# Four moves in a two-layer encoder kernel: gathers, query tables, gate weights, and a second attention unit

## The chip, the cores and the metric

The kernel runs on one core of one Trainium2 chip. A core has a matrix engine (TensorE; PE in the profile, its weight loads PEld), three engines for everything else (VectorE is DVE, ScalarE is ACT, GpSimd is POOL) and a queue for transfers on SyncE (SP). They work side by side, each through its own list of instructions in a fixed order, and wait for each other by semaphores. TensorE writes only to PSUM, eight banks; everything else lives in SBUF. The metric is the device time of one execution in microseconds, lower is better.

## The reference

The input is 1024 tokens of width 1024, with 16 learned meta tokens in front. Two layers follow: a gated linear attention (layer A), then attention over one shared, compressed key and value set (layer B).

```python
h = deltanet_layer(h, valid, ...)          # A: per 64 tokens, 8 heads of 128
#   o = rms_norm(o, o_gain) * silu(gate);  h = x + o @ w_out
c = rms_norm(h, g_norm) @ w_down           # shared latent: 256 latent + 64 rotary
k = rms_norm(concat(c_kv @ w_uk, k_pe)); k = concat(k_nope, rope(k_pe)); v = c_kv @ w_uv
# layer B
z = rms_norm(h, g_norm) @ w_in             # 384 query latent, 1024 gate
q = rms_norm(rms_norm(z[:384]) @ w_uq);    q = concat(q_nope, rope(q_rope))
o = softmax(mask(q @ k.T * scale)) @ v     # chunk-causal, 8 heads
h = h + (o * silu(z[384:])) @ w_out
```

All of it is in 32-bit floats. The kernel splits each operand of a large product into a high and a low part and makes three products of it (`mm3`, lines 92 to 95), so that lines 93, 94 and 95 are the three products wherever they stand.

## The kernel before

Activations are kept transposed, features on the partitions, tokens along the free axis, in the three token chunks of `TOKC`: 272, 384 and 384 tokens, the first with the meta tokens. Weights come in by `SY.dma_start` into a tile `raw` (or `rq`, `wdr`), and `split_w` makes the high part on GpSimd (line 100 or 106) and the low part on VectorE (101 or 107). `split_ps` does the same for a PSUM result, with ScalarE for the high part.

Layer A ends with eight gate blocks, one per head (`gate`, lines 776 to 784): three chunks of 24 products, a SiLU on ScalarE after each. The heads' outputs lie in DRAM (`o_scr`), 128 tokens to a tile, and have to be normalised, transposed, multiplied by the gates and split before the output projection can read them: `gather_rows` loads a tile's rows and gates, `out_gather` scales eight head pieces on ScalarE (line 761), transposes them on TensorE into two PSUM banks of the tag `tr` (767), multiplies by the gates (770, 772) and splits (773, 774). Tile -1 is the 16 meta tokens. The first three tiles (-1, 0, 1) make up the first token chunk `oT0`, and their gathers are handed to the last gate block as the list `between`: one after each chunk. The output projection (`out_project`) follows, chunk by chunk, with the gathers of later tiles among its blocks; these loads go to a pool that lies where `hT` was, so they wait until the last gate product has read it.

Then come the latent projections (from line 944): `latent_kv(c)` makes three blocks of products with `w_down` for chunk c, `latent_q(c)` three with the query part of `w_in`. Norms need a product with a matrix of ones (lines 1009 and 1039), whose result lies in the only bank of the tag `pt` until VectorE has read it (1011 and 1013, 1041). Work that waits for a norm is put off through the list `later` and called by `soon()` after the next block. Among it is `all_tables`: the rotary tables for queries (`qC`, `qS`, scaled) and, in place, for keys (`cosS`, `sinS`). The query weights come in eight pieces of 128 rows, fetched three ahead (`fetch_wq`) and split a pair at a time between the key blocks (`query_weights`). Behind `latent_kv(2)` the weights of the first gate block of layer B are loaded and split (`load_wg`), into space that the key weights leave.

The eight gate blocks of layer B (lines 1154 to 1170) are 48 products of 512 columns each. Blocks 1 to 7 take their weights from a pool of two buffers, which lies where the latent projections' tiles were, beside the up-projection weights of the first pair of heads (`pair_weights`).

The attention (from line 1173) is in a block opened with `tc.block(schedule_with_timeline_sim=True)`: the program's order is a priority, and a scheduler orders the instructions at compile time by estimated durations. It works by units of a pair of heads and 256 tokens, four units to a pair, 16 in all. `build` makes a unit's keys (`K`, a generator of five steps: projection and copy, squares, norm in three steps), values (`VV`), queries (`Q0`, `Q1`), their rotation on GpSimd (`R0`, `R1`) and the transposes of all of them (`TK`, `TR`, `turn_q`, `turn_qr`). All of these use three PSUM banks of the tag `bd`. `scores` makes a unit's products of queries and keys and the softmax, `weigh` the product with the values. `weave` interleaves several such generators by the estimates they yield, each between two shares of the span. Unit 0 is built by itself, then in each unit's scores the next unit is built, 0.8 of it beside the first head and the rest beside the second. The last output projection follows (`out_b`).

## Time and profile before

| what | us |
|---|---|
| median of 3 runs | 1327.56 |
| lowest and highest run | 1326.98, 1329.74 |
| profiled execution, device time | 1322.61 |
| its span, first to last instruction | 1320.9 |
| TensorE busy in it | 1281.3 |
| mean granted TensorE clock | 0.993 of full |

The profile is of one execution. The page lists busy time by engine, 40 slices of the span, the chain that ended last, and the costliest groups of instructions. Behind it stands the trace, which can be asked for waits, for the instructions of a stretch in order of time, and for the busy time of engines in a stretch. In order of time, a row is start, duration, engine, line, operation, tiles and shapes, how many, and in brackets how long the engine stood idle before and what released it. TensorE's durations overlap, since its products are pipelined; the pace is the difference of two starts. The granted clock is given as a share of 2.4 GHz.

### The profile page before, as it was taken

To read this page: it belongs to the slowest core of one execution; us is meant where nothing else is said; L and a number is where in the kernel's file an instruction comes from. 1 tells how busy PE (TensorE), PEld (TensorE's weight loads), DVE (VectorE), ACT (ScalarE), POOL (GpSimd) and SP (SyncE) were. 2 spreads that over 40 slices of the span, in tenths; PEclk is the share of its full clock that TensorE was granted. 3 is DMA by queue.
4 is the path that set the end of the run, shared out by engine and by line. 5 is a ranking of instruction groups with operands and counts; after the bars stand their busy time and mean duration, and the time that the engine had idled before them with its cause. 6 is when DMAs were issued, how large, how long until landed. Compare 5 with 4: busy or idle time off the path is not lost. (4 is left out here: it accounts for less than half of the span.)

```text
span 1320.9 us, 25401 instructions
## 1 busy us (share of the span) xinstructions
PE 1281.3 (97%) x9320; PEld 1196.2 (91%) x9320; DVE 901.6 (68%) x2534; ACT 598.3 (45%) x1764; POOL 320.0 (24%) x588
## 2 busy tenths in 40 slices
PE   6999999999999999999999999989999999998999
PEld 5889989989998999999999897878999999997888
DVE  7679789978987884653556655336878878777411
ACT  6543444344435422246522321137777777775200
POOL 3141121022111101040011013214544445447000
PEclk9999999999999999999999999999999999999999
DMA  5011111111111202174543004220101100014622
GB/s 198 33 34 46 52 29 54 41 45 40 57 49 37 64 24 91 61 241 147 178 127 104 11 18 144 81 90 15 53 25 50 43 29 26 21 40 165 203 90 79
DMA packets 95822, 96.85 MB, mean 73 GB/s; under 512 B 28526, under 2 KB 77614, under 8 KB 95698
## 3 DMA queue, kind: packets, MB, share of 16 engines
q1 hardware_dynamic: 95698, 95.23, 22.9%
q8 instruction: 73, 1.20, 0.4%
q14 instruction: 51, 0.42, 0.1%
HBM read 68.19 MB, written 27.01 MB: 72 GB/s over the span
## 5 line engine op out<-in xcount | busy, mean ns | idle before, releaser
L93 PE MATMUL mm<-hT_hi,whi 128*128 128x384 f32 (+1 forms) x768 | 255.5, 333 | 4.3 <-ACT hT_hi L293 4.3
L94 PE MATMUL mm<-hT_lo,whi 128*128 128x384 f32 (+1 forms) x768 | 254.9, 332 | 0.5 <-DVE hT_lo L294 0.5
L95 PE MATMUL mm<-hT_hi,wlo 128*128 128x384 f32 (+1 forms) x768 | 254.6, 332 | 0.0
L93 PEld LDWEIGHTS mm<-hT_hi,whi 128*128 128x128 f32 x768 | 146.2, 190 | 6.3 <-issue 5.5
L94 PEld LDWEIGHTS mm<-hT_lo,whi 128*128 128x128 f32 x768 | 146.4, 191 | 2.2 <-DVE hT_lo L294 1.0
L95 PEld LDWEIGHTS mm<-hT_hi,wlo 128*128 128x128 f32 x768 | 146.8, 191 | 1.1 <-issue 0.4
L100 POOL TENSOR_SCALAR whi<-raw 128x512 fp32r<-128x512 f32 x48 | 34.6, 736 | 165.8 <-PE mm L94 123.9
L93 PE MATMUL bd<-oTh,wf_hi 128*128 128x256 f32 (+1 forms) x192 | 61.4, 323 | 3.0 <-DVE xt L1610 3.0
L113 DVE TENSOR_TENSOR pTl<-pt,pTh 128x256 fp32r<-128x256 f32 (+2 forms) x112 | 54.7, 494 | 14.0 <-ACT pTh L112 12.8
L95 PE MATMUL bd<-oTh,wf_lo 128*128 128x256 f32 (+1 forms) x192 | 61.8, 322 | 0.0
L94 PE MATMUL bd<-oTl,wf_hi 128*128 128x256 f32 (+1 forms) x192 | 61.7, 322 | 0.0
L84 ACT ACTIVATE P<-P,mx 128x144 f32<-128x144 f32 (+3 forms) x64 | 50.6, 792 | 23.2 <-DVE mx L1448 15.0
L1610 DVE TENSOR_TENSOR xt<-bd,xt 128x256 f32<-128x256 f32 (+1 forms) x24 | 12.3, 514 | 67.9 <-PE bd L95 59.9
L396 ACT COPY z<-mm 128x384 f32<-128x384 f32 (+1 forms) x72 | 32.0, 444 | 58.3 <-PE mm L95 57.4
L1461 POOL TENSOR_SCALAR P<-P,sl 128x144 f32<-128x144 f32 (+3 forms) x64 | 52.4, 820 | 4.1
L112 ACT CAST pTh<-pt 128x256 fp32r<-128x256 f32 (+2 forms) x112 | 47.0, 427 | 12.8 <-DVE pTl L113 7.0
L101 DVE TENSOR_TENSOR wlo<-raw,whi 128x512 fp32r<-128x512 f32 x64 | 46.8, 741 | 8.4 <-POOL whi L100 8.3
L400 DVE SCALAR_TENSOR_TENSOR kn<-z,pcol,kn 128x384 f32<-128x384 f32 (+1 forms) x72 | 42.1, 585 | 15.2 <-ACT kn L398 14.3
L93 PE MATMUL sc<-h_hi,whi 128*128 128x512 f32 x128 | 50.8, 397 | 1.2 <-POOL whi L106 1.2
L95 PE MATMUL sc<-h_hi,wlo 128*128 128x512 f32 x128 | 50.6, 395 | 1.1 <-DVE wlo L107 1.1
L94 PE MATMUL sc<-h_lo,whi 128*128 128x512 f32 x128 | 50.6, 395 | 0.0
L93 PE MATMUL sc<-kn_hi,qn_hi 128*128 128x272 f32 (+3 forms) x160 | 48.0, 302 | 2.0 <-DVE mx L1448 1.5
(428 smaller groups left out, 4013.1 us busy)
## 6 DMA issues: line engine op xcount, KB each, us to landing
raw<-in_a_w_in SPq DMA_DIRECT2D x64, 256.0 KB
o_scr<-o SPq DMA_DIRECT2D x64, 64.0 KB
raw<-in_a_w_out SPq DMA_DIRECT2D x8, 512.0 KB
on<-o_scr SPq DMA_DIRECT2D x8, 512.0 KB
raw<-in_b_w_in SPq DMA_DIRECT2D x8, 512.0 KB
gb_scr<-z SPq DMA_DIRECT2D x8, 512.0 KB
gt<-gb_scr SPq DMA_DIRECT2D x32, 128.0 KB
ot_scr<-gt SPq DMA_DIRECT2D x32, 128.0 KB
```

The lines of the kernel that those rows point to most:

```text
L84: i = A.activation(out_ap, in_ap, func, **kw)
L93: TE.matmul(ps, ahi, bhi, start=first, stop=False)
L94: TE.matmul(ps, ahi, blo, start=False, stop=False)
L95: TE.matmul(ps, alo, bhi, start=False, stop=last)
L100: eng.tensor_scalar(out=hi, in0=raw, scalar1=1.0, scalar2=1.0, op0=ALU.mult, op1=ALU.mult)
L101: V.tensor_tensor(out=lo, in0=raw, in1=hi, op=ALU.subtract)
L112: A.copy(hi, ps)
L113: V.tensor_tensor(out=lo, in0=ps, in1=hi, op=ALU.subtract)
L396: A.copy(z[:, 3 + a:3 + b], gemm_T(hi, lo, c))
L400: V.scalar_tensor_tensor(out=yc, in0=z[:, a + j:b + j], scalar=col("cw", 24 * j + m), in1=yc, op0=ALU.mult, op1=ALU.add)
L1461: G.tensor_scalar(out=Pm[:, 0:n], in0=Pm[:, 0:n], scalar1=s, scalar2=1.0, op0=ALU.mult, op1=ALU.mult)
L1610: V.tensor_tensor(out=xt, in0=ps, in1=xt, op=ALU.add)
```

## The change

First, the gathers of tiles -1 and 0 both go behind the first chunk of the last gate block of layer A, that of tile 1 behind the second; behind the third there is none. Second, the tables for keys get tiles of their own (`kC`, `kS`) and stay at their place, the tables for queries are made behind `latent_q(0)`; the query weights are fetched two ahead instead of three, in two buffers, and the rotary temporaries `t1`, `t2` have one buffer instead of two. Third, the weights of the first two gate blocks of layer B are loaded and split behind `latent_kv(2)`, with one buffer for the raw weights, and blocks 2 to 7 use the other pool. Fourth, unit 0 of the attention is woven with the first part of unit 1 (`cut` at an estimate of 4100), for which `build` has an order of its own with values and queries first: by the estimates, `VV`, `Q0` and `Q1` fall into the opening, and the key steps and the rest come beside the scores of unit 0.

```diff
--- before.py
+++ after.py
@@ -821,7 +821,13 @@
 
         for t in (-1, 0, 1):
             gather_rows(t, so)
-        gate(H - 1, [first_gather(t) for t in (-1, 0, 1)])
+        gathers = [first_gather(t) for t in (-1, 0, 1)]
+
+        def first_two():
+            gathers[0]()
+            gathers[1]()
+
+        gate(H - 1, [first_two, gathers[2]])
 
 
     lps = ExitStack()
@@ -931,8 +937,8 @@
         V.memset(kpe[:, NT:NT + 1], 0.0)
         qC, qS = (cpool.tile([P, NT, ROPE], F32, name=x) for x in ("qC", "qS"))
 
-        def load_wg(pool, h):
-            raw = pool.tile([P, KT, P], F32, tag="raw", name=nm("raw"))
+        def load_wg(pool, h, raws=2):
+            raw = pool.tile([P, KT, P], F32, tag="raw", name=nm("raw"), bufs=raws)
             SY.dma_start(raw, I["b_w_in"][0].rearrange("(kt p) c -> p kt c", p=P)[:, :, QR + h * P:QR + (h + 1) * P])
             hi = pool.tile([P, KT, P], F32R, tag="whi", name=nm("whi"))
             lo = pool.tile([P, KT, P], F32R, tag="wlo", name=nm("wlo"))
@@ -965,28 +971,28 @@
                     V.tensor_tensor(out=S[:, :, x], in0=sinS[:, 0:n, x],
                                     in1=gr[:, gi:gi + 1, y].broadcast_to([P, n, hf]), op=ALU.mult)
 
-            def all_tables():
+            kC, kS = (wc.tile([P, NT + 1, ROPE], F32, name=x) for x in ("kC", "kS"))
+
+            def query_tables():
                 tables(qC, qS, 1, NT)
                 for x in (qC, qS):
                     V.tensor_scalar(out=x, in0=x, scalar1=QK ** -0.5, scalar2=None, op0=ALU.mult)
-                tables(cosS, sinS, 0, NT + 1)
-
-            kC, kS = cosS, sinS
+
             hf = ROPE // 2
             wqr = []
 
             def fetch_wq(kt):
-                wqr.append(sp.tile([P, WQ], F32, tag="rq", name=nm("rq"), bufs=3))
+                wqr.append(sp.tile([P, WQ], F32, tag="rq", name=nm("rq"), bufs=2))
                 SY.dma_start(wqr[kt], I["b_w_in"][0, kt * P:(kt + 1) * P, 0:QR])
 
             def query_weights():
                 for kt in range(KT):
                     split_w(wqr[kt], wq_hi[:, kt, :], wq_lo[:, kt, :], col("b", kt))
-                    if kt + 3 < KT:
-                        fetch_wq(kt + 3)
+                    if kt + 2 < KT:
+                        fetch_wq(kt + 2)
                     yield
 
-            for kt in range(3):
+            for kt in range(2):
                 fetch_wq(kt)
             wqs = query_weights()
 
@@ -1065,7 +1071,7 @@
                         continue
                     n, s0, i0 = len(ts), ts[0] % (NT + 1), tiles.index(ts[0])
                     s, x = slice(s0, s0 + n), pt[:k, i0:i0 + n]
-                    t1, t2 = (sp.tile([P, 3, ROPE], F32, tag=y, name=nm(y))[:k, 0:n] for y in ("t1", "t2"))
+                    t1, t2 = (sp.tile([P, 3, ROPE], F32, tag=y, name=nm(y), bufs=1)[:k, 0:n] for y in ("t1", "t2"))
                     V.tensor_tensor(out=t2, in0=x[:, :, 0:ROPE], in1=kC[:k, s, :], op=ALU.mult)
                     V.tensor_tensor(out=t1[:, :, 0:hf], in0=x[:, :, hf:ROPE], in1=kS[:k, s, 0:hf], op=ALU.mult)
                     V.tensor_tensor(out=t1[:, :, hf:ROPE], in0=x[:, :, 0:hf], in1=kS[:k, s, hf:ROPE], op=ALU.mult)
@@ -1097,7 +1103,7 @@
                 V.tensor_tensor(out=kp, in0=ps, in1=rrow[0:ROPE, a:b], op=ALU.mult)
                 soon()
                 if c == 0:
-                    later.append(all_tables)
+                    later.append(lambda: tables(kC, kS, 0, NT + 1))
                 later.append(lambda: rotary(c, kp))
 
             def latent_q(c):
@@ -1114,9 +1120,11 @@
             latent_kv(0)
             latent_kv(1)
             latent_q(0)
+            query_tables()
             latent_kv(2)
             lwd.close()
-            wg0 = load_wg(lpre.enter_context(tpool(name="wg0", bufs=1, side="right")), 0)
+            wg0 = lpre.enter_context(tpool(name="wg0", bufs=2, side="right"))
+            first_gates = [load_wg(wg0, h, 1) for h in range(2)]
             latent_q(1)
             latent_q(2)
             soon()
@@ -1154,7 +1162,7 @@
         with ExitStack() as lg:
             wg = lg.enter_context(tpool(name="wg", bufs=2))
             for h in range(H):
-                hi, lo = wg0 if h == 0 else load_wg(wg, h)
+                hi, lo = first_gates[h] if h < 2 else load_wg(wg, h)
                 z = wg.tile([P, T], F32, tag="z", name=nm("z"))
                 for half in range(2):
                     c = slice(512 * half, 512 * half + 512)
@@ -1232,7 +1240,7 @@
             return first, second, third
 
 
-        def build(u, w, r):
+        def build(u, w, r, early=False):
 
             uk_hi, uk_lo, uv_hi, uv_lo, uq_hi, uq_lo = w
             base = NM if u == 0 else 0
@@ -1245,7 +1253,7 @@
             kn_hi, kn_lo, kr = (kt_(x, [P, 2, NM + 256], KB) for x in ("kn_hi", "kn_lo", "kr"))
             v_hi, v_lo = (kt_(x, [P, 2, 2, P], KB) for x in ("v_hi", "v_lo"))
             qn_hi, qn_lo, qr_hi = (kt_(x, [P, 2, 256], QB) for x in ("qn_hi", "qn_lo", "qr_hi"))
-            qr_lo = r["qr_lo"] = qr_lows[len(units) % 2]
+            qr_lo = r["qr_lo"] = qr_lows[(r["n"] + 1) % 2]
             qsc = kt_("qsc", [P, 2, 2], QB, F32)
             tiles = (2 * u, 2 * u + 1)
             main = dict(tiles=tiles, c0=base, k=P, s0=2 * u)
@@ -1408,6 +1416,10 @@
             VV, TK, TR = (lambda: values(main)), (lambda: turn_keys(main)), (lambda: turn_rotary(main))
             pieces = ((1284, K), (1284, K, VV), (60, K), (1444, K, Q0), (60, K, R0), (430, TK), (1444, Q1), (60, R1),
                       (430, TR, q1), (430, q2_, turn_q), (430, q3, neg, turn_qr))
+            if early:
+
+                pieces = ((1284, VV), (1444, Q0), (1444, Q1), (1284, K), (60, K), (60, K), (60, K, R0), (60, K),
+                          (430, TK), (60, R1), (430, TR, q1), (430, q2_, turn_q), (430, q3, neg, turn_qr))
             for t, *fs in pieces:
                 for f in fs:
                     f()
@@ -1547,21 +1559,23 @@
         def started(n):
 
             p, g = seq[n]
-            units[p, g] = {}
-            return build(g, wts[p], units[p, g])
+            units[p, g] = {"n": n}
+            return build(g, wts[p], units[p, g], n == 1)
 
 
         sc_t = lambda g: 1070 * (g + 1)
         wg_t = lambda g: 1070 * (g + 1) + 600
         bd_t = lambda g: 7300 + (2000 if g == 0 else 0)
 
-        weave((started(0), 1, 0, 1))
+        FILL = 4100
+        second = started(1)
+        weave((started(0), bd_t(0), 0, 1), (cut(second, FILL), FILL, .1, .8))
         last, lt_ = None, 1
         for n, (p, g) in enumerate(seq):
             us = [units[p, u] for u in range(g + 1)]
             new, total = None, 1
             if n + 1 < len(seq):
-                new, total = started(n + 1), bd_t(seq[n + 1][1])
+                new, total = (second, bd_t(1) - FILL) if n == 0 else (started(n + 1), bd_t(seq[n + 1][1]))
             for j in range(2):
                 extra, Ps = None, []
                 if j == 1 and g == NU - 2 and p + 1 < H // 2:
```

## Rows read from the trace of the kernel before

**Rows 1.** The page's first part: busy us, share of the span, instructions, by engine.
```profile
PE 1281.3 (97%) x9320; PEld 1196.2 (91%) x9320; DVE 901.6 (68%) x2534; ACT 598.3 (45%) x1764; POOL 320.0 (24%) x588
```

**Rows 2.** TensorE's waits: line, what it waited for: us in total, times, longest.
```profile
PE bd L1284 <- DVE kk L1317: 5.0, 3, 2.6
```

**Rows 3.** Instructions in order of time: start, us, engine, [idle before], around the last gate block.
```profile
606.18 0.42 PE L93 MATMUL mm<-hT_hi,whi 128*128 128x384 f32 x1
...
607.41 1.35 DVE L774 TENSOR_TENSOR oT0l<-gtile,oT0h 128x512 fp32r<-128x512 f32 x2
...
610.45 1.04 PE L767 MATMUL tr<-ident,on 128*128 128x128 f32 x8
613.12 0.90 PE L93 MATMUL sc<-oT0h,wo_hi 128*128 128x272 f32 x5 [1.63 <-ACT oT0h L773]
...
614.17 2.46 ACT L761 ACTIVATE on<-on,ro 128x128 f32<-128x128 f32 x8 [0.58 <-DMA on<-o_scr]
...
619.74 1.04 PE L767 MATMUL bd<-ident,on 128*128 128x128 f32 x8
```

**Rows 4.** In order of time: latent keys of the first two token chunks, query weights.
```profile
718.87 1.05 DVE L965 TENSOR_TENSOR qS<-sinS,gr 128x256 f32<-128x256 f32 x2
...
719.86 0.62 PE L1039 MATMUL pt<-ssb,ones 128*128 128x272 f32 x2
720.21 1.38 DVE L107 SCALAR_TENSOR_TENSOR wq_lo<-rq,pcol,wq_hi 128x384 fp32r<-128x384 f32 x2
...
721.87 0.42 DVE L1041 SCALAR_TENSOR_TENSOR rsh<-pt,vrow 128x272 f32<-128x272 f32 x1
...
722.34 0.91 PE L1009 MATMUL pt<-ssx,ones 128*128 128x384 f32 x2 [0.96 <-DVE rsh L1041]
...
723.54 2.96 POOL L106 TENSOR_SCALAR wq_hi<-rq,pcol 128x384 fp32r<-128x384 f32 x3 [2.89 <-DMA rq<-in_b_w_in]
...
733.17 0.62 DVE L107 SCALAR_TENSOR_TENSOR wq_lo<-rq,pcol,wq_hi 128x384 fp32r<-128x384 f32 x1
...
736.29 0.58 PE L93 MATMUL sc<-h_hi,wq_hi 128*128 128x256 f32 x1
```

**Rows 5.** In order of time: gate blocks 0 to 2 of layer B.
```profile
792.60 1.75 SPq L936 DMA_DIRECT2D raw<-in_b_w_in  x2
...
800.22 6.97 POOL L106 TENSOR_SCALAR whi<-raw,pcol 128x128 fp32r<-128x128 f32 x16 [0.53 <-PE sc L95]
...
801.37 0.50 PE L93 MATMUL sc<-h_hi,whi 128*128 128x512 f32 x1 [1.21 <-POOL whi L106]
...
803.23 0.51 PE L95 MATMUL sc<-h_hi,wlo 128*128 128x512 f32 x1 [1.13 <-DVE wlo L107]
...
814.03 0.39 PE L93 MATMUL sc<-h_hi,whi 128*128 128x512 f32 x1
```

**Rows 6.** Stretches (length, busy us and instructions by engine, clock, DMA), then order of time.
```profile
883.02:884.43 1.41, 1.41 (x14) 1.38 (x13) 1.15 (x7) 1.37 (x3) 0.00 (x0) 1.00 0.87 320
885.54:887.20 1.66, 1.66 (x9) 1.51 (x9) 0.37 (x3) 1.60 (x8) 0.00 (x0) 1.00 0.81 234
892.18:895.24 3.06, 3.06 (x10) 2.74 (x9) 0.58 (x2) 0.19 (x1) 0.00 (x0) 0.50 0.00 0
880.90:898.40 17.50, 12.78 (x70) 10.49 (x68) 9.44 (x36) 10.83 (x38) 3.34 (x8) 0.80 0.33 110
898.40:912.30 13.90, 12.11 (x88) 11.33 (x89) 10.21 (x35) 10.69 (x43) 7.35 (x18) 1.00 0.00 0
912.00:1225.00 313.00, 304.88 (x2451) 298.37 (x2452) 251.68 (x800) 229.49 (x727) 153.21 (x279) 1.00 0.16 51
...
886.57 0.56 ACT L112 CAST v_hi<-bd 128x512 fp32r<-128x512 f32 x1
...
888.74 0.45 ACT L1353 COPY qraw<-bd 128x384 f32<-128x384 f32 x1
...
907.49 0.63 PE L1284 MATMUL bd<-ident,kk 128*128 128x128 f32 x4 [1.29 <-DVE kk L1317]
```

## The prediction

> **What bounds the kernel now.** I read the busy shares first. TensorE is busy 1281.3 of the 1320.9 us [rows 1], so what is left to gain is the 39.6 us in which it stands still, and whatever it does at half clock. No part of the change removes a matmul. So the next view is that of TensorE's waits: the one on `kk`, 5.0 us in three waits, is the opening of the attention [rows 2], and the other waits that the change touches show in the order of time: 1.63 us where the last gather meets the first output projection [rows 3], 0.96 us at a matrix product of ones ahead of the second token chunk's norms [rows 4], 1.21 and 1.13 us at the start of the second gate block of layer B [rows 5]. Last come the stretches of the opening: in 880.90 to 898.40 TensorE works 12.78 of 17.50 us at a mean granted clock of 0.80, in 898.40 to 912.30 12.11 of 13.90 us [rows 6]. These four places sum to 4.93 us of waits outside the attention and 6.51 us of idle time in its opening, plus what the clock costs there.
>
> **Gathers between chunks.** Nothing is added or removed: the transposes of tile 1 (8 of them, 1.04 us) move from behind the third chunk of the last gate block to ahead of it, those of tile 0 from ahead of that chunk to ahead of the second one. Before, their evictions lie open: transposes from 610.45, the first projection matmul at 613.12 after 1.63 us of waiting, and then with five first products ahead because the low half is still missing [rows 3]. A chunk lasts 4.27 us (606.18 to 610.45). The same evictions for tile 0, started at about 606, are done by 608.76 on VectorE, so a chunk covers them. What is late next: the rows of tile 2, whose loads wait for the last matmul on `hT`. That matmul comes about 1.0 us later (the transposes that now precede it), so their scaling on ScalarE, 614.17 to 616.63 now, ends near 617.7, while two projection blocks from about 611.6 (613.12 to 619.74 now is 6.6 us) want them near 618. That can cost 0 to 0.5 us. Gain 1.63 less about 0.1: I take **1.5**, between 1.0 and 1.8.
>
> **Query tables later, two buffers for the query weights.** The product with ones at 719.86 waits for nothing, but VectorE reads its result only at 721.87, behind the two sine products of the query table (1.05 us) and two weight splits (1.38 us); the next product with ones needs that one PSUM bank and waits 0.96 us [rows 4]. With the query table out of that place the reader comes up to 1.05 us earlier, which is all of the wait. The query operations go behind the first query block, where VectorE waits for TensorE most of the time; but the kernel's scheduler may still pull them forward, since their inputs are there, and then nothing is won. The key tables write new tiles instead of overwriting, which costs no operation. The fetches of query weights go from three buffers to two. The splits on GpSimd start at 717.5 (three), 723.54 after 2.89 us without data, and so on; the last low half ends at 733.79, and TensorE first reads these weights at 736.29 [rows 4]. In pairs a round is the wait for data (up to 2.89 us) plus two splits (2.96 us for three, so 2.0): 4.9 us; the fourth pair begins at 717.5 + 14.7 = 732.2 and its low halves end near 735. Pairs are used in order, the last ones some 2 us after 736.29, so this is hidden with 1 to 3 us to spare; behind a late split VectorE's norms queue, so a late round could cost up to 2 us. I take a gain of **0.7**, between 1.2 and a loss of 2.0.
> The Trainium skill speaks against fewer buffers: "DMA: Bandwidth & Descriptors", section "Anatomy of one DMA", gives about 2.0 us per transfer that does not shrink with size (fitted on the GpSimd path; these go over SyncE's queue). With its size term, 192 KB would be an estimated 2.4 us, and the row's 2.89 us without data agrees; by the page the three waits of the four rounds would end the splits about 1.4 us sooner than by the row, so the gain of 0.7 stays either way.
>
> **Two gate blocks' weights ahead.** The wait at the second gate block is for its weights: the loads of blocks 1 and 2 are issued at 792.60 with the pair weights ahead of them, the splits start at 800.22, and TensorE, done with block 0, waits 1.21 us for the high and 1.13 us for the low half [rows 5]. After, block 1's load goes out once block 0's only raw buffer is split, and its 8 splits (6.97/16 = 0.44 us each, 3.5 us) run beside two query blocks. SyncE's queue holds that load behind a wait, and nothing is queued behind it there before the loads at 792.60 and the pair weights just ahead of them. What is late next is block 2: its load is then the first at 792.6, its splits start near 800.2 and end near 804 to 806, and it is wanted only after block 1, which takes 12.6 us now (801.37 to 814.03, waits included) and would start at 800.2. Gain 2.34 plus the slower first products after each wait (0.1 to 0.2): **2.4**, between 2.0 and 2.6; nothing of block 1 can be late any more.
>
> **Part of the second unit in the opening.** Moved are one value projection (12 products, 1.41 us) and two query projections (9 products, 1.66 us each) of unit 1, 4.7 us of TensorE in all, into the first unit's build [rows 6]. Their evictions move too: 0.56 us and twice 0.45 us on ScalarE, the low half of the values on VectorE. Before, the first unit stands alone: it waits for its key norms, and the query projection that follows runs at half clock (9 products in 3.06 instead of 1.66 us, granted clock 0.50: the 1.2 GHz level). Worked out in four terms. First, with products of unit 1 in the wait the clock should not fall: 1.4 gained, I take 1.3. Second, the new evictions queue on ScalarE ahead of the squares of unit 0's keys: 1.5 us, of which I count 0.9 as lost, since ScalarE has idle time later in the stretch. Third, behind the opening the key chain of unit 1 (projection to transposes at 907.49) was covered by just the work that now leaves; the chain itself becomes shorter by what it no longer queues behind (0.56 + 0.45 on ScalarE, a bit on VectorE: 1.2). TensorE will wait there longer than 1.29 us, but the chain ends sooner. Fourth, the second query projection no longer stands between the key transposes and the query transposes: 1.6. Sum 1.3 - 0.9 + 1.2 + 1.6 = **3.2**. Upper end: all of the moved 4.7 plus the clock's 1.3, 6.0. Lower end: the 1.5 of ScalarE and 0.7 of VectorE delay unit 0 in full and nothing comes back, a loss of 2.2. I stand in between because the stretch is a chain of small steps, not a queue of work.
>
> **Sum.** 1.5 + 0.7 + 2.4 + 3.2 = 7.8 us. The profiled execution took 1322.61 us (span 1320.9 and 1.7 around it), so it would become 1314.8. It lies 4.95 us under the median of the runs, 1327.56; I take the difference over to that median: **1319.8 us**.
>
> **The rivals.**
> *The opening fills completely.* The order leaves no bubble behind it: 6.0 instead of 3.2, so 10.6 in all, 1317.0. For it: 6.51 us idle in both stretches. Against it: three PSUM banks for all projections and transposes of a build, and a key chain of over 6 us with little left to cover it.
> *The opening only moves its wait.* Unit 1's key chain lies bare by as much as was filled before: 0 from this part, 4.6 in all, 1323.0. For it: the 1.29 us wait is there already while 4.7 us of cover still stand.
> *The change does not do what it says.* The scheduler pulls the query tables forward, the rows of tile 2 or the query weights come late, and the opening loses: 1.0 - 2.0 + 2.4 - 1.4, about nothing, 1327.6. For it: each has its row. Against it: the gate block's 2.34 us depend on nothing else.
> *Slower, by one mechanism:* the attention is ordered by a scheduler at compile time, and a changed opening lets it plan all that follows anew. From 912 to 1225 TensorE is idle only 8.12 of 313 us [rows 6], with 14 units still to be built. If each of them lost the 1.79 us that 898.40 to 912.30 loses, that would be 25 us, 17 more than now, and the result 1336.8. It decides the sign from 10.5 us of new idle time (7.8 and the 2.7 us of 0.2%), 0.75 us a unit. Against it: from the third unit on there are scores of earlier units to fill with, and the program's order there is unchanged.
>
> **How the numbers follow.** Forecast 0.56; filled completely 0.14; wait only moved 0.14; nothing 0.10; slower 0.06. The range reaches from a sum of 13 (every part at its upper end and a little of the following stretch, 1314.5) to a sum of 1.6 (1326.0); outside it lie the slower case, nearly all of "nothing", and a few hundredths below. A measurement of this kernel can tell about 0.2%, 2.7 us, from no change. Faster by more than that: forecast, filled and most of the moved wait, 0.82. Within it: 0.12. Slower: 0.06.
>
> **What would show it.** In the profile after: the first output projection follows the last gate product with under 0.3 us of idle time; no wait at the second gate block, and none at the third; the product with ones near 722 waits under 0.3 us; the granted clock of the opening's query projections is 1.0, and the first scores of unit 1 start 3 us earlier counted from the last gate product of layer B. Wrong would be: a wait on `wq_lo` or `wq_hi` near 736, a wait on the key transposes of unit 1 of over 4 us, or more than 12 us of idle TensorE in the rest of the attention.

## The result

The changed kernel takes 1321.34 us, median of 8 runs (1316.44 to 1325.02), beside 1327.45 for the kernel before (8 runs, 1326.05 to 1332.97). That is 6.1 us less by the medians, where 7.8 were forecast, and inside the range. The ratio on record, which is not that of the two medians, is 0.9942, 95% interval 0.9923 to 0.9960: 7.7 us less, between 5.3 and 10.2. The profiled execution after took 1320.28 us, with a span of 1318.5 and a mean granted clock of 0.988.

The two profiled executions differ by 2.3 us only. That is no contradiction, as a table by stage shows; each stage runs from the start of its first named instruction to that of the next (the last one to the end of the span).

| stage, us | before | after | gain | forecast |
|---|---|---|---|---|
| start to the first gather transposes of the last gate block | 600.50 | 603.59 | -3.09 | 0 |
| to the first output projection product | 12.62 | 10.80 | 1.82 | 1.5 |
| to the first product with ones of the latent stage | 97.24 | 97.09 | 0.15 | 0 |
| to the first gate product of layer B | 77.81 | 77.79 | 0.02 | 0.7 |
| to the first key product of the attention | 92.74 | 89.84 | 2.90 | 2.4 |
| to the first scores of unit 1 | 31.40 | 31.28 | 0.12 | 3.2 |
| to the end | 408.55 | 408.15 | 0.40 | 0 |

The first line is code that was not touched. In the 14 profiles of this study it takes 600.50 to 605.91 us, and the granted clock in it differs from profile to profile (0.98 to 0.99); the kernel before happens to have the shortest. So the profiles are compared by stage and the times by the runs. The gains behind that line sum to 5.4 us, near the runs' 6.1.

The page of after, its first part (busy us, share, instructions) and the granted clock in 40 slices; against [rows 1] the same work, in a shorter span:

```profile
PE 1284.6 (97%) x9320; PEld 1199.6 (91%) x9320; DVE 902.6 (68%) x2534; ACT 598.6 (45%) x1764; POOL 319.3 (24%) x588
...
PEclk8999999999998999999999999998999999999999
```

TensorE's waits after (line, what it waited for: us in total, times, longest). The row of [rows 2] is down from 5.0 to 0.7 us, and the waits of [rows 3] and [rows 5] are no longer in the list. Two rows are new or larger: a wait for a PSUM bank that the eviction `v_lo` holds, and waits for the row maxima `mx`:

```profile
PE sc L93 <- DVE mx L1460: 2.7, 4, 0.9
...
PE bd L93 <- DVE v_lo L113: 1.6, 1, 1.6
...
PE pt L1015 <- DVE rsh L1047: 0.8, 1, 0.8
...
PE bd L1292 <- DVE kk L1325: 0.7, 1, 0.7
```

In order of time (start, us, engine, line, tiles), the end of the last gate block after, beside [rows 3]: the transposes of tile 1 stand ahead of the third chunk, and the projection follows the last gate product 0.18 us later, at the pace of the products, with no wait:

```profile
609.33 1.03 PE L767 MATMUL tr<-ident,on 128*128 128x128 f32 x8
...
614.21 0.34 PE L95 MATMUL mm<-hT_hi,wlo 128*128 128x384 f32 x1
614.39 0.29 PE L93 MATMUL sc<-oT0h,wo_hi 128*128 128x272 f32 x1
```

And the passage from gate block 0 to gate block 1 of layer B after, beside [rows 5]: the starts keep their distance of 0.23 us.

```profile
800.18 0.40 PE L95 MATMUL sc<-h_hi,wlo 128*128 128x512 f32 x1
800.41 0.40 PE L93 MATMUL sc<-h_hi,whi 128*128 128x512 f32 x1
```

### The profile page after: what moved, and what is told of

The parts are those of the page before. It is cut to its first block, busy times and chain, and to the rows that moved or that the text cites. A ratio compares the mean times of both kernels' runs of the same rounds, so it can differ in the third digit from the quotient of the medians.

```text
span 1318.5 us, 25399 instructions
## 1 busy us (share of the span) xinstructions
PE 1284.6 (97%) x9320; PEld 1199.6 (91%) x9320; DVE 902.6 (68%) x2534; ACT 598.6 (45%) x1764; POOL 319.3 (24%) x588
## 4 chain that ended last, share of the span: by engine, by line
PE 82%; DVE 5%; ACT 3%; DMA 3%; issue 2%; POOL 2%; SPq 0%; DVEq 0%; ACTq 0%; POOLq 0%
PE mm L93 9%; PE mm L94 9%; PE mm L95 9%; PE sc L93 7%; PE sc L94 7%; PE sc L95 7%; PE bd L93 4%; PE bd L95 4%; PE bd L94 4%; PE pt L1502 2%; PE tr L508 1%; PE ch L640 1%; PE tr L500 1%; PE ch L650 1%; PE ch L636 1%
## 5 line engine op out<-in xcount | busy, mean ns | idle before, releaser
L1502 PE MATMUL pt<-ident,P 128*128 128x128 f32 x288 | 47.7, 281 | 3.5 <-DVE pm L1494 1.9
```

The source lines that it names most:

```text
L1502: TE.transpose(pt[:, kb, x * P:(x + 1) * P], Ps[x][0][:, y0 + kb * P:y0 + (kb + 1) * P], ident)
```

## The experiments

### Each part alone

Four kernels carry one part of the change each, on the kernel before. All four ran beside the same runs of the kernel before (median 1329.02). Of each edit the lines that matter are shown; "..." stands for the others.

```diff
-        gate(H - 1, [first_gather(t) for t in (-1, 0, 1)])
...
+        gate(H - 1, [first_two, gathers[2]])
```

> Only the first part: the gathers of tiles -1 and 0 behind the first chunk of the last gate block, that of tile 1 behind the second. Theory, from the traces of before and after: the stretch from the first of these transposes to the first output-projection product falls from 12.6 to 10.8 us, all else stays, so 1.8 us less in all (about 1325.6 where before is 1327.4). The forecast had 1.5. Rival: the rows of tile 2, loaded 1 us later, make the projection wait, and the first token chunk of the projection (the time to the last of its 64 products of each kind) grows by over 0.5 us.

Ratio 0.9996 (0.9983 to 1.0010). The stage of the gathers takes 10.80 us as in the changed kernel, against 12.62 in the three other kernels: the 1.82 us are there each time. They don't arrive in the time. In its profile the gate stage, whose code is that of the kernel before, takes 94.12 us at a clock of 0.98 instead of 92.74 at 1.00, and the attention is ordered otherwise: unit 1's first scores come 34.45 us behind the first key product, not 31.40.

```diff
-                tables(cosS, sinS, 0, NT + 1)
...
+            kC, kS = (wc.tile([P, NT + 1, ROPE], F32, name=x) for x in ("kC", "kS"))
...
+            query_tables()
             latent_kv(2)
```

> Only the second part: query tables behind the first query block, two buffers for the query weights. Theory: nothing, since the scheduler pulls the query products forward to where they were: the wait at the product with ones near 722 stays at 0.8 to 1.0 us, and the stretch from the first key-latent product to the first gate product stays at 77.6 us. Rival, the forecast: the wait goes and the stretch is 0.7 us shorter. A second rival: with two buffers the query weights come late, a wait near 736 and a stretch up to 2 us longer.

Ratio 1.0003 (0.9987 to 1.0019). The stage takes 77.79 us beside 77.81: next to nothing gained, nothing lost.

```diff
-                hi, lo = wg0 if h == 0 else load_wg(wg, h)
+                hi, lo = first_gates[h] if h < 2 else load_wg(wg, h)
```

> Only the third part: the weights of two gate blocks ahead. Theory: both waits at the second block (1.21 and 1.13 us) go, and none comes up at the third; the stretch from the first gate product of layer B to the first key product of the attention falls from 92.7 to 89.8 us, 2.9 us less in all (about 1324.5). The forecast had 2.4. Rival: part of the 2.9 us comes from the other parts (the pool for the rotary temporaries and fetches lies elsewhere), then 2.3 or less is seen here.

Ratio 0.9958 (0.9941 to 0.9975), the one part that shows by itself. Its gate stage takes 89.84 us, to the hundredth what the changed kernel has.

```diff
-        weave((started(0), 1, 0, 1))
+        FILL = 4100
+        second = started(1)
+        weave((started(0), bd_t(0), 0, 1), (cut(second, FILL), FILL, .1, .8))
```

> Only the fourth part: part of unit 1 in the attention's opening. Theory: the wait is only moved. From the first key product of the attention to the first scores of unit 0 stays at 17.6 us, to the first scores of unit 1 at 31.3 (31.4 before), the clock is 1.00 in the opening's query projections and falls to about 0.6 behind unit 0's scores; the time is that of before within 0.5 us. Rival, the forecast: the first scores of unit 1 come 3.2 us earlier after the first key product (28.2) and the time is 3.2 us less.

Ratio 0.9989 (0.9959 to 1.0020): 1.5 us by the middle, and the interval holds no change as well as the 3.2 of the forecast. By stage, unit 1's first scores come at 30.32 instead of 31.40 us, between the theory (31.3) and the forecast (28.2), the end at 439.86 instead of 439.95 from the first key product.

### The query tables held back

```diff
-            query_tables()
+            with tc.issue_after(behind[-1].ins):
+                query_tables()
             latent_kv(2)
```

> The changed kernel with one edit: the query tables may not be ordered ahead of the last sum of squares of the first query block. Theory (the tables' part gained nothing because the scheduler pulled the query products forward, in front of the reader of the product with ones): the wait at that product falls from 0.82 us to under 0.3, and the stretch from the first product with ones to the first gate product, 77.8 us in the changed kernel, becomes 76.9 to 77.3. Rival (the two weight splits in front of the reader hold it, with or without the tables): the wait stays between 0.6 and 1.2 us and the stretch at 77.6 or more. In both the time moves by less than can be measured: 1319 to 1322 us beside 1321.3.

The first theory holds. Time 1320.34 us, ratio 0.9934 (0.9894 to 0.9975), which can't tell it from the changed kernel; the stage tells: 77.14 instead of 77.79 us. VectorE and TensorE in the changed kernel: in the program's order the query tables stand behind `latent_q(0)`, and yet `qS` runs at 719.40 and 721.10, ahead of two splits and of the reader `rsh`, which starts at 722.84:

```profile
719.40 0.73 DVE L971 TENSOR_TENSOR qS<-sinS,gr 128x256 f32<-128x256 f32 x1
720.05 1.12 DVE L971 TENSOR_TENSOR kS<-sinS,gr 128x288 f32<-128x288 f32 x2
721.10 0.41 DVE L971 TENSOR_TENSOR qS<-sinS,gr 128x256 f32<-128x256 f32 x1
721.43 1.13 DVE L107 SCALAR_TENSOR_TENSOR wq_lo<-rq,pcol,wq_hi 128x384 fp32r<-128x384 f32 x2
...
722.84 0.42 DVE L1047 SCALAR_TENSOR_TENSOR rsh<-pt,vrow 128x272 f32<-128x272 f32 x1
...
723.32 0.91 PE L1015 MATMUL pt<-ssx,ones 128*128 128x384 f32 x2 [0.82 <-DVE rsh L1047]
```

The same place with the tables held back: counted from the stage's first product with ones, at 711.48 and 711.60, the splits start 1.2 us earlier and the reader 0.9 us, and the next product with ones waits for nothing:

```profile
719.09 0.82 DVE L971 TENSOR_TENSOR kS<-sinS,gr 128x288 f32<-128x288 f32 x2
720.31 1.46 DVE L107 SCALAR_TENSOR_TENSOR wq_lo<-rq,pcol,wq_hi 128x384 fp32r<-128x384 f32 x2 [0.41 <-POOL wq_hi L106]
...
722.04 0.42 DVE L1049 SCALAR_TENSOR_TENSOR rsh<-pt,vrow 128x272 f32<-128x272 f32 x1
...
722.52 0.91 PE L1015 MATMUL pt<-ssx,ones 128*128 128x384 f32 x2
```

Two further kernels with this edit (below) have 76.98 and 77.10 us in this stage, the seven with the tables moved but without it 77.63 to 77.86, the four with the tables where they were 77.81 to 78.11.

### The opening: bank or key chain

What the opening of the changed kernel looks like, TensorE's rows in order of time (idle time in front of a row in brackets); the first key product is at 879.11:

```profile
886.63 0.44 PE L93 MATMUL bd<-uqh,cqT 128*128 128x384 f32 x1 [1.61 <-DVE v_lo L113]
...
891.42 0.82 PE L1292 MATMUL bd<-ident,kk 128*128 128x128 f32 x6
...
896.73 0.33 PE L93 MATMUL sc<-kn_hi,qn_hi 128*128 128x144 f32 x1 [0.59 <-ACT qn_hi L115]
...
903.13 0.48 PE L1491 MATMUL pt<-ident,Pe 128*128 128x128 f32 x1 [1.08 <-POOL Pe L1471]
905.91 1.12 PE L1292 MATMUL bd<-ident,kk 128*128 128x128 f32 x4 [0.68 <-DVE kk L1325]
```

The key transposes of unit 0 (891.42) wait for nothing any more, as forecast, but a query projection waits 1.61 us for a bank, and unit 0's first scores come 17.62 us behind the first key product, before 17.55. By stretch (length, busy us and instructions of PE, PEld, DVE, ACT, POOL, then clock, DMA share, GB/s), after and then the changed kernel profiled a second time (`c4_changed_again`, below):

```profile
889.11:896.71 7.60, 6.38 (x38) 5.23 (x36) 2.35 (x8) 5.07 (x18) 3.58 (x11) 1.00 0.01 4
896.71:903.11 6.40, 4.72 (x33) 4.10 (x33) 4.99 (x18) 4.88 (x21) 3.38 (x9) 1.00 0.00 0
903.11:910.41 7.30, 6.49 (x30) 5.33 (x30) 6.14 (x23) 5.52 (x23) 2.84 (x7) 0.53 0.01 2
879.11:910.41 31.30, 25.98 (x162) 22.69 (x160) 20.23 (x77) 22.83 (x83) 9.80 (x26) 0.89 0.19 62
```
```profile
898.17:904.57 6.40, 6.15 (x33) 5.51 (x33) 4.14 (x14) 4.00 (x17) 2.96 (x8) 0.73 0.00 0
904.57:911.87 7.30, 5.56 (x23) 4.44 (x24) 6.17 (x25) 6.05 (x26) 3.19 (x8) 0.57 0.00 0
880.57:911.87 31.30, 26.50 (x155) 23.23 (x154) 19.40 (x75) 22.48 (x82) 9.75 (x26) 0.84 0.19 61
```

Before, the slow stretch was ahead of unit 0's scores: 17.50 us at a mean clock of 0.80 [rows 6], so 2 x 0.20 x 17.5 = 7.0 us at the 1.2 GHz level. After, it is behind them: 2 x 0.47 x 7.30 = 6.9 us. The same amount, in another place: what it costs there is worked out below, with the four terms.

```diff
-                split_ps(project(c, uv_hi, uv_lo), v_hi, v_lo)
+                split_ps(project(c, uv_hi, uv_lo, "pt" if early else "bd"), v_hi, v_lo)
...
-                ps = bank2("bd", [P, 512])
+                ps = bank2("sc" if early else "bd", [P, 512])
```

> The changed kernel with one edit: the moved projections of unit 1 write to PSUM banks that stand empty in the opening (tags pt and sc) and not to the three of tag bd. Theory (the key chain of unit 1 is what ends last behind the opening): the wait of 1.61 us for a bank in the opening goes, TensorE stands still as long further on, and from the first key product the first scores of unit 1 come at 30.5 to 31.3 us (31.28 in the changed kernel), the last scores of the attention at 327.5 to 329. Rival (the bank is what the opening lost): the first scores of unit 0 come at 16.0 to 16.5 instead of 17.62, those of unit 1 at 29.5 to 30, the last ones at 326 to 327.5, and the time is 1.5 to 2 us below that of the changed kernel.

Both were half right. The bank wait goes and unit 0's first scores come at 16.22 us, 1.40 earlier, so the bank did cost that. Unit 1's come at 30.57, only 0.71 earlier, and the end is 440.71 us behind the first key product, between the 439.43 and 441.97 of the changed kernel's two profiles (the second one is below): a gain to the end does not show. Median 1322.89 us, ratio 0.9940 (0.9915 to 0.9965), as the changed kernel.

```diff
-                pieces = ((1284, VV), (1444, Q0), (1444, Q1), (1284, K), (60, K), (60, K), (60, K, R0), (60, K),
+                pieces = ((1284, K), (1284, VV), (60, K), (1444, Q0), (60, K), (1444, Q1), (60, K, R0), (60, K),
...
-        FILL = 4100
+        FILL = 5600
```

> The changed kernel with another order of what is moved into the opening: the keys of unit 1 first, then its values and queries between the steps of the key chain, cut at an estimate of 5600 instead of 4100. Theory (the opening's gain was lost to the key chain of unit 1, which starts only behind unit 0's scores): the chain is now done when unit 0 is scored, no wait on key transposes is left behind 20 us from the first key product, the granted clock there is over 0.95, and the first scores of unit 1 come at 27 to 29 us instead of 31.28. The last scores of the attention come at 325.5 to 327.5 instead of 328.72. Rival (the opening is a queue on VectorE and ScalarE, and what goes into it delays unit 0 by as much): the first scores of unit 0 come at 19 to 20.5 us instead of 17.62, those of unit 1 at 30.5 to 32, and the last at 328 to 329.5.

(The early unit's `kk` gets a buffer of its own for this.) The rival's picture: unit 0's first scores at 19.39 us, unit 1's at 32.50, and a wait of 2.77 us on the key transposes of unit 1. Median 1321.95 us, ratio 0.9929 (0.9903 to 0.9956); the end comes 439.89 us behind the first key product.

The edits of the two kernels together:

> The edits of the two kernels before together: the keys of unit 1 first, and its values and queries in banks of their own. Theory (key chain first, bank second): the first scores of unit 1 at 26.5 to 28.5 us from the first key product, the last of the attention at 325 to 327, time 2 to 4 us below the changed kernel. Rival (VectorE's and ScalarE's queue): as for the kernel with the keys first alone, within 0.5 us: banks change nothing.

Unit 1's first scores come at 29.49 us, 1.8 earlier than in the changed kernel but later than the theory had them, and the end at 436.61 (439.43 and 441.97 in the changed kernel's two profiles). The time, median 1319.97 us and ratio 0.9916 (0.9889 to 0.9943), can't be told from the changed kernel's. With keys first the bank matters after all: without the banks the same order gave 32.50. What is left is the wait on the key transposes, and its cause shows on ScalarE: the keys of unit 1 are copied at 887.12, but their squares run from 898.21, behind everything of unit 0, 11 us later.

```profile
887.12 0.57 ACT L1314 COPY kk<-bd 128x512 f32<-128x512 f32 x1
...
898.21 0.31 ACT L84 ACTIVATE junk<-kk 128x128 f32<-128x128 f32 x1
...
903.62 1.08 PE L1292 MATMUL bd<-ident,kk 128*128 128x128 f32 x4 [3.29 <-DVE kk L1328]
```

### The opening undone, and what can be had

These four ran together (kernel before: median 1329.53). In the first the fourth part is undone:

```diff
-        FILL = 4100
-        second = started(1)
-        weave((started(0), bd_t(0), 0, 1), (cut(second, FILL), FILL, .1, .8))
+        weave((started(0), 1, 0, 1))
```

> The changed kernel with its fourth part undone: gathers, tables and gate weights as changed, the opening as before. Theory (behind the opening nearly all of its gain is given back): from the first key product to the end 439.9 to 440.9 us, as in the four kernels with the opening as before, beside 439.4 in the changed kernel; the time is 0 to 1.5 us above the changed kernel's. Rival (the opening brings the 3.2 us of the forecast, and the landmark of unit 1's first scores hides it): 2.5 to 4 us above the changed kernel. In both the stretches ahead of the attention are those of the changed kernel: 10.8, 77.8 and 89.84 us.

Ratio 0.9955 (0.9939 to 0.9971), beside 0.9946 for the changed kernel that ran with it: the fourth part is worth 0.0009, 1.2 us, in the middle (0.3 by the medians, 1323.28 and 1322.99), which is the theory's size; the two intervals overlap, so the rival's 2.5 us and more is not excluded by the times. The stages ahead of the attention are as expected (10.80, 77.72, 89.84). The end, at 444.50 us, missed both expectations. Part of that lies in the opening: unit 1's first scores come at 35.56 us, in the order of work that the kernels with the gathers or the gates alone have too (34.45 and 34.26), and not in that of the kernel before (31.40). The clock was 0.96 in the last 124 us, beside 0.98 in the kernel before and 0.99 and 0.97 in the changed kernel's two profiles.

```diff
+            with tc.issue_after(behind[-1].ins):
+                query_tables()
...
+                pieces = ((1284, K), (1284, VV), (60, K), (1444, Q0), (60, K), (1444, Q1), (60, K, R0), (60, K),
```

> Keys of unit 1 first, banks of their own for its values and queries, and the query tables held back behind the last sum of squares. Theory (the gains lie in different places and add up): first product with ones to first gate product 77.1 us, first key product to end 436 to 438, time 3 to 4 us below the changed kernel, 1317 to 1318 where that has 1321. Rival (the gain to the end was an accident of the scheduler's order): the attention is ordered anew, first key product to end 438.5 to 440.5, time within 1.5 us of the changed kernel.

(With the banks of their own for the values and queries of unit 1, and the cut at 5600.) By stage the gains add up: 76.98 us in the latent stage, the end at 437.00 us. The time doesn't show it as clearly: median 1321.01 us, ratio 0.9926 (0.9905 to 0.9946), below the changed kernel that ran with it by 2.7 us by the ratios and 2.0 by the medians, with intervals that overlap.

```diff
-                pieces = ((1284, K), (1284, VV), (60, K), (1444, Q0), (60, K), (1444, Q1), (60, K, R0), (60, K),
+                pieces = ((1344, K, K), (1284, VV), (1444, Q0), (60, K), (1444, Q1), (60, K), (60, K, R0),
...
-        weave((started(0), bd_t(0), 0, 1), (cut(second, FILL), FILL, .1, .8))
+        weave((started(0), bd_t(0), 0, 1), (cut(second, FILL), FILL, .25, .9))
```

> As the kernel before, and the squares of unit 1's keys follow right behind their projection in the program's order, the moved part between shares 0.25 and 0.9 of the span. Theory (with the keys first, ScalarE ran the squares of unit 1 only behind all of unit 0, 11 us after the copy, and that made the wait of 3.3 us on the key transposes): the wait falls below 1.5 us, no stretch at half clock over 4 us, first scores of unit 1 at 27 to 28.5 us, first key product to end 434.5 to 436.5. Rival (the squares only take their place ahead of unit 0's work, which comes later by as much): first scores of unit 0 at 18.5 to 20 instead of 17.1, first key product to end 437 to 439.

(On top of the edits of the kernel before it.) Median 1315.23 us, ratio 0.9904 (0.9881 to 0.9926), whose interval lies below that of the changed kernel (0.9929 to 0.9963): the fastest of all. The wait on the key transposes is gone (905.22), and unit 1's first scores come at 28.35 us, as the theory had it, with unit 0's still at 17.10. Two smaller waits stand in its place, and the stretch behind unit 0's scores still runs at half clock, which the theory had not; the end of the profiled execution, one of the two slowest of its six, is at 438.46 us, above what the theory had and inside what the rival had (437 to 439):

```profile
900.27 0.49 PE L1461 MATMUL sc<-kr,qr_hi 128*128 128x144 f32 x1 [1.45 <-POOL qr_hi L1417]
...
902.85 0.49 PE L93 MATMUL sc<-kn_hi,qn_hi 128*128 128x144 f32 x1 [1.33 <-DVE mx L1466]
...
905.22 1.05 PE L1295 MATMUL bd<-ident,kk 128*128 128x128 f32 x4
```
```profile
897.73:904.13 6.40, 3.62 (x15) 2.81 (x15) 4.62 (x22) 5.64 (x28) 2.50 (x7) 0.52 0.00 0
```

> The changed kernel itself, beside the three others on the same chip: 1319.5 to 1322.5 us, and the same order of instructions and the same stretches as in its first profile (10.8, 77.8, 89.84 us, first key product to end within 1 us of 439.4). What its stretches differ by between two profiles is the error of all comparisons by stretch.

Median 1322.99 us, just above the expected range, ratio 0.9946 (0.9929 to 0.9963). The stages ahead of the attention repeat within 0.1 us. The attention does not: the end comes at 441.97 instead of 439.43 us, the first scores of unit 1 at 32.20 instead of 31.28. The waits are those of the first profile within 0.05 us up to unit 0's scores; what differs is the clock, 0.73 instead of 1.00 in the 6.40 us behind them (fences above). So a stage of the attention can't be read closer than 1 us at its opening and 2.5 us over its whole length from one profile.

## Why the prediction was right, and where it was not

**The sign and the size.** Faster, 6.1 us of 7.8, inside the range. Of the four terms two came out larger, two nearly vanished: by stage, gathers and gates gave 4.7 us where 3.9 were forecast, tables and opening 0.1 where 3.9 were forecast. That the sum came out so near is in part luck. By its mechanism this is the rival of the moved wait (4.6 us in all, 1323.0), with the tables lost and larger gains at the gathers and the gates; the measured 1321.34 lies midway between that rival and the forecast.

**Gathers: right.** 1.82 us instead of 1.5, in every kernel with this part. What was feared next, the rows of tile 2, cost nothing: the output projection takes 97.09 us, before 97.24. That the part alone did not show in the time is no contradiction: its interval reaches to 0.9983, 2.3 us.

**Gates: right, with a mis-sized term.** The two waits of [rows 5] sum to 2.34 us, yet 2.90 came back. The kernel before, around the two waits:

```profile
799.76 0.40 PE L95 MATMUL sc<-h_hi,wlo 128*128 128x512 f32 x1
...
801.71 0.40 PE L94 MATMUL sc<-h_lo,whi 128*128 128x512 f32 x1
...
803.58 0.40 PE L93 MATMUL sc<-h_hi,whi 128*128 128x512 f32 x1
```

The pace is 0.23 us, but a wait is counted from the modelled end of the product before, 0.40 us after its start. From 799.76 to 801.37 are 1.61 us, 1.38 over the pace; then 0.34 (0.11 over), 1.52 (1.29 over) and 0.35 (0.12 over): 2.90. The prediction had the slower first products (0.1 to 0.2) but not the 0.16 or so that the overlap hides in each wait. The gathers fit this: 1.82 for a wait of 1.63.

**Tables: the gain failed on a step that the prediction had named.** "The kernel's scheduler may still pull them forward, since their inputs are there, and then nothing is won": that is what happened, and the product with ones waits 0.82 instead of 0.96 us. The size was right: held back, they give 0.65 us of the forecast 0.7. The two buffers cost nothing; the last low half ends at 736.1 and no wait on these weights shows. For the fetches, GpSimd stood without data for 3.65, 3.20 and 2.15 us ahead of the later rounds, where the prediction had taken 2.89 [rows 4]. The Trainium skill ("DMA: Bandwidth & Descriptors", section "Anatomy of one DMA") gives a transfer a fixed part of about 2.0 us, fitted on another path than SyncE's queue. The prediction's estimate of 2.4 us by it lies between these gaps. Since the weights came in time, neither changes the result.

**Opening: the rival that it only moves its wait.** Of the forecast 3.2 us, 0.12 came, and in the second profile of the same kernel a loss of 0.80. The first two terms reach up to unit 0's scores, the last two from there to unit 1's. The rows that the four terms are read from, before and then after:

```profile
898.46 0.34 PE L93 MATMUL sc<-kn_hi,qn_hi 128*128 128x144 f32 x1 [0.48 <-ACT qn_hi L115]
...
899.24 0.38 PE L93 MATMUL bd<-ukh,ckvT 128*128 128x256 f32 x1
...
910.30 0.60 PE L1284 MATMUL bd<-ident,qraw 128*128 128x128 f32 x4
...
912.31 0.37 PE L93 MATMUL sc<-kn_hi,qn_hi 128*128 128x272 f32 x1
```
```profile
892.17 0.44 PE L93 MATMUL bd<-uqh,cqT 128*128 128x384 f32 x1
...
897.52 0.39 PE L93 MATMUL bd<-ukh,ckvT 128*128 128x256 f32 x1
...
907.03 1.06 PE L1292 MATMUL bd<-ident,qraw 128*128 128x128 f32 x4
...
910.39 0.37 PE L93 MATMUL sc<-kn_hi,qn_hi 128*128 128x272 f32 x1
```

*First, the clock: right at its place.* The query projections no longer run at half clock. From the second query projection of unit 0 to its first scores (892.18 to 898.46 before, 892.17 to 896.73 after) it takes 4.56 us instead of 6.28: 1.72 gained where 1.3 were counted.

*Second, the evictions: twice the loss, on another path.* That projection starts 1.79 us later, counted from the first key product, where 0.9 were counted as lost. The prediction had the new evictions ahead of the squares of unit 0's keys on ScalarE. In the trace the squares come first, and the evictions queue behind them; until the values are evicted their bank stays taken, and TensorE waits for it. `v_lo` ends at 886.57, and the query projection starts at 886.63:

```profile
884.89 0.31 ACT L84 ACTIVATE junk<-kk 16x128 f32<-16x128 f32 x1
...
885.29 0.56 ACT L112 CAST v_hi<-bd 128x512 fp32r<-128x512 f32 x1
...
885.88 0.69 DVE L113 TENSOR_TENSOR v_lo<-bd,v_hi 128x512 fp32r<-128x512 f32 x1 [0.22 <-ACT v_hi L112]
```

The kernel with banks of their own had 1.40 us of it back. So unit 0 was to be scored 1.3 - 0.9 = 0.4 us earlier, and came 0.07 later.

*Third, the key chain of unit 1: wrong.* It was to be 1.2 us shorter. From its projection to its transposes it takes 905.91 - 897.52 = 8.39 us, before 907.49 - 899.24 = 8.25: not shorter at all, and it begins where it began, 0.79 us behind unit 0's first scores (0.78 before). The wait in front of the transposes is 0.68 us, where one of more than 1.29 was forecast.

*Fourth, the second query projection of unit 1: right at its place, and lost behind it.* From the key transposes to the query transposes it takes 907.03 - 905.91 = 1.12 us instead of 910.30 - 907.49 = 2.81: 1.69 gained where 1.6 were counted. But from there to unit 1's first scores it takes 3.36 us instead of 2.01. After, TensorE works at about half clock all the way from the key transposes to these scores; before, it did more in about the same time at full clock. The two stretches, before and then after:

```profile
907.49:912.31 4.82, 4.42 (x33) 4.12 (x33) 3.38 (x9) 3.17 (x11) 3.82 (x10) 1.00 0.00 0
```
```profile
905.91:910.39 4.48, 4.48 (x25) 4.48 (x25) 4.10 (x15) 2.78 (x8) 0.87 (x2) 0.55 0.01 4
```

At full clock the 4.48 us of products would take about 4.48 x 0.55 = 2.5 us, an estimate that leaves out what else might then be waited for. So the half clock that the first term had taken off came back behind unit 0's scores and took back what the fourth had gained; the prediction had no term for that. In all 1.72 - 1.79 - 0.01 - 0.14 + 0.34 = 0.12.

In the kernel with the keys first, banks of their own, and the squares right behind the projection, the wait on the key transposes is gone, and unit 1's first scores come at 28.35 instead of 31.28 us. Several things differ between the two kernels: the order, the banks, and how much is moved. The keys first without the banks gave 32.50, the banks without the order 30.57, so neither does it alone. That the head of the chain is what counts fits these numbers, but no run changes it by itself.

**The slower rival.** The attention was planned anew, but not dearer. Kernels whose opening is that of the kernel before show unit 1's first scores at 31.39, 34.26, 34.45 and 35.56 us, before 31.40; to the end it is 440.2 to 440.9 in three of them, before 439.95. From 912 to 1225 TensorE is idle 7.6 us after (305.44 busy of 313), 8.1 before [rows 6]; this rival decides the sign only from 10.5 us more.

**What the clock of the runs explains, and what stays open.** The gate part alone brought 0.9958, at least 3.3 us by its interval, where its stage gives 2.9; the profiles show no place for the rest. The runs do: there are only four of this kernel, with a mean granted clock of 0.990, where the kernel before has 0.987 over the 25 runs beside them. Over the 59 runs of these five kernels, a straight line with one slope for all kernels gives 0.84 us more for each 0.001 of clock less, an estimate. At equal clock the four parts then stand, beside the kernel before, at 1.5 us less (gathers), 0.2 more (tables), 3.3 less (gates) and 0.6 less (opening), each give or take 1.5 us, the gates 2.2. That agrees with the stages.

What the opening is worth stays open. Undoing it gives 1.2 us by the ratios and doing it alone 1.5, and either can be 0 or 3; at equal clock they are 0.2 and 0.6. The gain of the kernel with the squares first is not of this kind: at equal clock it is 5.5 us, give or take 1.9, below the changed kernel.

## What to carry to other kernels

Where a scheduler orders the instructions, moving an operation back in the program need not move it back on its engine. Here only an ordering edge did, and the trace shows at once whether it moved. Filling a wait with a neighbour's work can move the wait and the half clock behind it instead of removing them, so follow both to the next landmark. What helped here was to fill with the head of the neighbour's longest chain and to give the filling work buffers that nothing else wants. Size a removed wait by the starts of the instructions around it against their pace, not by the wait's own row. Before a difference of a few runs is put down to the code, compare their granted clocks.

## What the runs showed of the hardware

The granted clock falls without any long wait: after, in 903.11 to 910.41 TensorE was busy 6.49 of 7.30 us with no wait above 1.1 us, and ran at 0.53; just ahead of it, from 896.71 to 903.11, it had run at 1.00, busy 4.72 of 6.40 us, with two waits, of 0.59 and 1.08 us. The Trainium skill ("TensorE: Matmul & The Clock Gate", section "A second HAM failure mode: psum-queue depth-cycling") reports a kernel, cycling through PSUM banks, in which frequent small idle times between groups of products make the clock swing between its two levels; these stretches agree. The same program got 0.73 or 1.00 in the same stretch in two executions, and untouched code of 600 us took 600.50 to 605.91 us.
